# Moving the renewal of the residual stream from GpSimd to VectorE, and reordering the start of a mixer, in a two-layer trunk on one Trainium2 core

## The chip, the cores and the metric

The kernel runs on one core of one Trainium2 chip. The metric is the device time of one execution in microseconds (us). Five engines work side by side: PE (TensorE, matrix products), DVE (VectorE), ACT (ScalarE), POOL (GpSimd) and SP (SyncE, which issues the DMA transfers of the weights).

## The reference, cut to what matters

```
for layer in range(2):
    shift, scale, gate = ada_modulation(c, ada_w[layer, 0], ada_b[layer, 0])
    h = x * (1.0 + scale) + shift
    y = mixer_ab(h, ...) if layer == 0 else mixer_c(h, ...)
    x = layer_norm(DN_ALPHA * x + gate * y, ln_g[layer, 0], ln_b[layer, 0])
    shift, scale, gate = ada_modulation(c, ada_w[layer, 1], ada_b[layer, 1])
    h = x * (1.0 + scale) + shift
    y = squared_relu_mlp(h, mlp_w1[layer], mlp_w2[layer])
    x = layer_norm(DN_ALPHA * x + gate * y, ln_g[layer, 1], ln_b[layer, 1])
```

There are 256 tokens of width 1024, all in float32. `mixer_c` is causal attention over queries, keys and values that one projection `c_w_in` gives (16 heads of 64). The MLP is 1024 to 4096 to 1024. `ada_modulation` multiplies the vector c with a 1024 x 3072 matrix, four times in all.

## The kernel before

The tokens are two blocks b of 128. Every product of the trunk is float32 in three passes (`mm3`, L232 to L236): both factors are split into a high and a low part, ACT makes the high part by a cast (`wh`, `hTh`, `uh`, L171) and DVE the low one by a subtraction (`wl`, `hTl`, `ul`, L172).

**Weights.** `plan` is one list of keys of 1 MB each: `w1` and `w2` of an MLP, `ci` the input projection of mixer C (`ci` 0 and 1 queries of the first head group, 2 and 3 keys, 4 and 5 values), `ada` the modulation matrices. SP loads them in this order into four places. `take` consumes the next key: a weight is split, in two halves, into places for three keys; an `ada` key is two products on DVE (`ada_product`, L320, tile `junk`), with no work for PE. `need(key)` takes up to a key, `ahead(n)` takes n weights further. `LATER` moves single instructions earlier (negative) or later in the order that the scheduler writes for each engine; an engine runs its list in order.

**An MLP** (`mlp`, L911) has 16 steps i. Step i makes hidden units from `w1` (`first`) and adds the last step's to four accumulators in PSUM with `w2` (`second`), which for MLP 0 keeps products of block 1 back for its finish.

**Between two stages** each block b goes through `residual` (L570 to L572: z from the accumulator, gate and x, and its statistics), `moments` (a reciprocal root on POOL, L300) and `norm` (L587). PE transposes z (`ps_mod`, L421); ACT (L426) and for half of block 1 DVE (L429) evacuate it with scale and shift into `h`; ACT and DVE split it into `hTh` and `hTl`, which the next stage's products read. In `renew` (between MLP 0 and mixer C) this is written out in L596 to L608; after a mixer `mixed_out` does it beside the output products. The next residual needs x itself: `new_x` (L589) makes it from z with the LayerNorm's gain and shift (`lngB`, `lnbB`), in four multiplications and four additions of 128x512 on POOL, straight behind the norms. This happens three times: after mixer 0, after MLP 0 and after mixer C.

**Mixer C starts** with `c_project(0)` (L998): queries of blocks 0 and 1, then keys of blocks 0 and 1, then values.

Of the kernel before, what the change touches and what calls it, by code (L numbers as in the profile page):

```python
# [42 lines left out]
NSPLIT = 6  # L43

SPLITS_LATER, ADA_LATER, ROWS_LATER = 200, 300, 0
LATER = {("co", 1, 1): -300, ("wo", 2, 0): 400, ("ada", 1, 5): 500, "cM1": 30, "cO011": -300, "cO100": 100, "s1": -300, "wO010": 30, "wO110": -40, "wY10": -80}

BESIDE = {"a0": [2, 2, 2, 2], "a1": [2, 2, 2, 2], "b0": [2, 2, 2, 2], "c10": [3, 1, 1, 1]}

# [13 lines left out]
def trunk(ctx: ExitStack, tc, c, x, pos, small, ln, ada, w_g, w_g1, w_uq, w_out, c_in, c_out, w1, w2, out):  # L63
# [39 lines left out]
    def ada_ss(i):  # L103
        return [("ada", i, k) for k in range(8)]

    def ada_g(i):
        return [("ada", i, 8 + j) for j in range(4)]
# [5 lines left out]
        "ada_1_4 ada_1_5 ada_1_6 ada_1_7"  # L113
    ).split()]

    def mlp_plan(l, more):

        more, p = list(more), [("w1", l, 0)]
        for i in range(16):
            p += ([("w1", l, i + 1)] if i < 15 else []) + [("w2", l, i)]  # L120
            if i >= 2:
                take = -(-len(more) // 8)
                p += more[:take]
                more = more[take:]
        assert not more
        return p

    plan += mlp_plan(0, ada_g(1) + ada_ss(2) + ada_g(2))
    plan += [("ci", j) for j in range(6)]
    for j in range(6):  # L130
        plan += [("ci", 6 + j)] + ada_ss(3)[j:j + 1]
    plan += [("co", 0)] + ada_ss(3)[6:] + [("co", j) for j in (1, 2, 3)]
    plan += mlp_plan(1, ada_g(3))
    place = {key: i for i, key in enumerate(plan)}

    source = {"ada": lambda i, o: ada[i, o], "g": lambda k: w_g[k], "g1": lambda k: w_g1[k], "uq": lambda: w_uq,
# [32 lines left out]
    def split(dh, dl, src):  # L169

        nc.scalar.copy(dh, src)  # L171
        nc.vector.tensor_sub(dl, src, dh.bitcast(F32))  # L172

    def take():

        key = plan[state["taken"]]
        w = raw.get(key)
        if w is None:
            pass
        elif key[0] == "uq":  # L180
            parts[key] = [w[:, :1024], w[:, 1024:]]
        elif by_tensor(key):
            with later(ROWS_LATER):
                ada_rows(key, w)
        elif key[0] == "ada":
            j = state["half"]
            with later(LATER.get(key, ADA_LATER)):
                state["half"] = ada_product(key, j, w[:, j * D:(j + 1) * D])
            if state["half"]:
                return  # L190
        else:
            cuts = (0, 1024, 2048)
            parts[key] = []
            for part, (lo, hi) in enumerate(zip(cuts, cuts[1:])):
                if key in (("wo", 0), ("co", 0)):
                    if lo == 0:
                        wide = [t.rearrange("p k q -> p (k q)") for t in new_hT()]
                    wh, wl = wide[0][:, lo:hi], wide[1][:, lo:hi]
                else:
                    wh = sp.tile([P, 1024], F32R, name="wh", tag="wh")[:, :hi - lo]  # L200
                    wl = sp.tile([P, 1024], F32R, name="wl", tag="wl")[:, :hi - lo]
                half = (*key, part)
                with later(LATER.get(half, SPLITS_LATER)):
                    split(wh, wl, w[:, lo:hi])
# [237 lines left out]
    def rope(src, heads, b, dsts, eng=nc.vector):  # L442

        t1 = work.tile([P, 8, HD], F32, name="rope1", tag="r2", bufs=8)[:, :heads]
        t2 = work.tile([P, 8, HD], F32, name="rope2", tag="r2", bufs=8)[:, :heads]
        cs = cosT[:, b:b + 1, :].to_broadcast([P, heads, HD])
        lo = sinT[:, b:b + 1, :32].to_broadcast([P, heads, 32])
        hi = sinT[:, b:b + 1, 32:].to_broadcast([P, heads, 32])
        eng.tensor_mul(t1, src, cs)
        eng.tensor_mul(t2[:, :, :32], src[:, :, 32:], lo)  # L450
        eng.tensor_mul(t2[:, :, 32:], src[:, :, :32], hi)
        for d, view in dsts:
            eng.tensor_add(d, view(t1), view(t2))
# [110 lines left out]
    def new_z():  # L564
        return work.tile([P, D], F32, name="z", tag="w4", bufs=2), col([P, 2, 6], "stats")
# [21 lines left out]
            nc.vector.tensor_scalar(z[:, s], z[:, s], mv[:, 0:1], rs, op0=ALU.subtract, op1=ALU.mult)  # L587

    def new_x(zs, gb):  # L589
        for b in range(NB):  # L590
            for h in range(2):
                s = slice(h * 512, (h + 1) * 512)
                nc.gpsimd.tensor_mul(xt[b][:, s], zs[b][0][:, s], gb[0][:, s])
                nc.gpsimd.tensor_add(xt[b][:, s], xt[b][:, s], gb[1][:, s])

    def renew(finish, gb, i):  # L596

        need(("ada", i, 7))
        zs = [new_z() for b in range(NB)]
        hT = new_hT()  # L600
        for b in range(NB):
            finish(b, zs[b])
            norm(b, zs[b])
            modulate(zs[b][0], b, i, hT)
            if b == 0:
                ahead(1)
        new_x(zs, gb)
        return hT  # L608


    xT = [work.tile([P, 4, 256], F32, name=f"xT{h}", tag="w4", bufs=2) for h in range(2)]
# [233 lines left out]
    def mixed_out(ys, name, i, first, second, under_first, under_second, after):  # L845

        yT, accs, zs, got = [None, None], {}, {}, {}  # L850
        got["ln"] = ln_rows(i)

        def step(s):
            op, *n = s
            b = int(n[0]) if n else 0
            if op in todo:
                with later(LATER.get(s, 0)):
                    todo[op](b)
            if op == "Y":
                if n[1] == "0":  # L860
                    yT[b] = new_yT(b)
                with later(LATER.get(name[0] + s, 0)):
                    y_half(ys[b], yT[b], int(n[1]))
                if n[1] == "1":
                    zs[b] = new_z()
            elif op == "O":
                h, kq = int(n[1]), int(n[2])
                if (b, h) not in accs:
                    accs[b, h] = pa("ps_out")
                need((name, 2 * h + kq))  # L870
                with later(LATER.get(name[0] + s, 0)):
                    out_part(accs[b, h], yT[b], (name, 2 * h + kq), kq, kq == 0, kq == 1)
            elif op == "G":
                with later(LATER.get(name[0] + s, 0)):
                    got["gate"] = gate_row(i)
            elif op == "R":
                with later(LATER.get(name[0] + s, 0)):
                    residual(b, int(n[1]), accs[b, int(n[1])], got["gate"], zs[b])
            elif op == "N":
                with later(LATER.get(name[0] + s, 0)):  # L880
                    norm(b, zs[b])
            elif op == "M":
                if b == 0:
                    need(("ada", i + 1, 7))
                    got["h"] = new_hT()
                with later(LATER.get(name[0] + s, -100)):
                    modulate(zs[b][0], b, i + 1, got["h"])

        def go(todo):
            for group in todo.split("|"):  # L890
                for s in group.split():
                    step(s)
                yield

        together(first, go(under_first))
        together(second, go(under_second))
        together(go(after))

        def rest():
            step("M1")  # L900
            new_x([zs[0], zs[1]], got["ln"])

        return got["h"], rest

# [5 lines left out]

    def mlp(l, hT, rest, rows):  # L911
        held = l == 0
        acc = [[(pd if b else pa)("ps_m2") for h in range(2)] for b in range(NB)]
        us = {}

        def first(i):
# [9 lines left out]
            ul = work.tile([P, 512], F32R, name="ul", tag="r2", bufs=8)  # L926
            nc.scalar.activation(r, ps, AF.Relu)
            nc.scalar.activation(r, r, AF.Square)
            split(uh, ul, r)
            us[i] = uh, ul  # L930

        def first_tokens(i, b):
# [28 lines left out]
        need(("w1", l, 1))  # L961
        for i in range(2):
            first_tokens(i, 0)
        rest()
        for i in range(2):
            first_tokens(i, 1)
        for i in range(16):
            if i >= 1:
                need(("w2", l, i - 1))
            if i > 1:  # L970
                first(i)
            if i == 10:
                gB, gb = rows()
            if i < 15:
                need(("w1", l, i + 1))
            if 1 <= i < 15:
                for b in range(NB):
                    for h in range(2):
                        if not (held and b and i == 14):
                            second(i - 1, b, h)  # L980
# [11 lines left out]
        return finish, gb  # L992

    finish, gb = mlp(0, hT, rest, lambda: (gate_row(1), ln_rows(1)))
    hT = renew(finish, gb, 2)


    ys = [work.tile([P, D], F32, name=f"y{b}", tag="w4", bufs=2) for b in range(NB)]  # L998
# [1 line left out]
    def c_project(g, got):  # L1000
# [121 lines left out]
```

## Time and profile before

| | |
|---|---|
| time, median of 3 | 679.63 us (678.79 to 680.69) |
| the profiled execution | 681.17 us, span 679.4 us |
| granted clock of PE, mean | 0.979 of full speed |
| busy: PE, DVE, ACT, POOL | 640.7, 470.8, 339.8, 74.4 us |
| DMA queue of the weights | 150.71 MB, 60.8% of 16 engines |

The profile is of one execution; its span leaves out 1.8 us around the program. The stages lie as follows: mixer 0 up to about 150 us, MLP 0 up to 341, mixer C from there up to about 480, MLP 1 up to about 665, and the last LayerNorm. In the rows below an entry in brackets is the idle time of the engine ahead of the instruction, and what ended it.

### The profile page before, as it was taken

To read this page: it belongs to the slowest core of one execution; us is meant where nothing else is said; L and a number is where in the kernel's file an instruction comes from. 1 tells how busy PE (TensorE), PEld (TensorE's weight loads), DVE (VectorE), ACT (ScalarE), POOL (GpSimd) and SP (SyncE) were. 2 spreads that over 40 slices of the span, in tenths; PEclk is the share of its full clock that TensorE was granted. 3 is DMA by queue.
4 is the path that set the end of the run, shared out by engine and by line. 5 is a ranking of instruction groups with operands and counts; after the bars stand their busy time and mean duration, and the time that the engine had idled before them with its cause. 6 is when DMAs were issued, how large, how long until landed. Compare 5 with 4: busy or idle time off the path is not lost.

```text
span 679.4 us, 9863 instructions
## 1 busy us (share of the span) xinstructions
PE 640.7 (94%) x3802; PEld 531.7 (78%) x3802; DVE 470.8 (69%) x859; ACT 339.8 (50%) x538; POOL 74.4 (11%) x93
## 2 busy tenths in 40 slices
PE   6999988998999999999959999999999999999994
PEld 3545766876898989899847887888788989898983
DVE  2859877278888778665687889864986744445437
ACT  3326656264645554555443554782655454555440
POOL 4010003044020000000051000002410000000004
PEclk8999989999999999999977999999999999999997
DMA  8992678406798978775344775830568675545301
GB/s 304 409 414 103 211 265 326 192 4 244 276 380 306 352 271 316 294 291 206 110 173 155 277 291 212 304 124 1 177 215 312 246 254 184 198 157 190 113 1 62
DMA packets 24385, 151.52 MB, mean 223 GB/s; under 512 B 2833, under 2 KB 3089, under 8 KB 8338
## 3 DMA queue, kind: packets, MB, share of 16 engines
q1 hardware_dynamic: 24194, 150.71, 60.8%
q8 instruction: 30, 0.49, 0.3%
q10 hardware_dynamic: 144, 0.18, 0.1%
q14 instruction: 17, 0.14, 0.1%
HBM read 149.83 MB, written 1.05 MB: 222 GB/s over the span
## 4 chain that ended last, share of the span: by engine, by line
PE 75%; DVE 7%; issue 7%; DMA 5%; ACT 2%; POOL 2%; SPq 0%; DVEq 0%; POOLq 0%; ACTq 0%
PE ps_m L236 17%; PE ps_m L234 17%; PE ps_m L235 17%; PE ps_s L491 3%; PE ps_c L236 3%; PE ps_c L235 3%; PE ps_c L234 3%; PE ps_pv L510 3%; DMA w_ada<-in_ada_dram 3%; DVE wl L172 2%; PE ps_pt L503 2%; DMA w_g<-in_w_g_dram 2%; PE ps_ada L340 1%; DMA early<-in_ada_dram 1%; PE ps_T L469 1%
## 5 line engine op out<-in xcount | busy, mean ns | idle before, releaser
L172 DVE TENSOR_TENSOR wl<-w_w,wh 128x1024 fp32r<-128x1024 f32 x128 | 157.3, 1248 | 93.2 <-ACT wh L171 92.6
L171 ACT CAST wh<-w_w 128x1024 fp32r<-128x1024 f32 x128 | 131.1, 1052 | 154.7 <-PE ps_m L235 89.0
L234 PE MATMUL ps_m<-hTh,wh 128*128 128x256 f32 x448 | 126.7, 283 | 0.0
L236 PE MATMUL ps_m<-hTh,wl 128*128 128x256 f32 x448 | 126.7, 283 | 0.0
L235 PE MATMUL ps_m<-hTl,wh 128*128 128x256 f32 x448 | 126.6, 283 | 0.0
L234 PE MATMUL ps_m<-wh,uh 128*128 128x512 f32 x256 | 101.9, 399 | 0.0
L235 PE MATMUL ps_m<-wl,uh 128*128 128x512 f32 x256 | 101.4, 396 | 0.2 <-DVE wl L172 0.2
L236 PE MATMUL ps_m<-wh,ul 128*128 128x512 f32 x256 | 101.2, 397 | 0.0
L320 DVE CUSTOM_DVE_ANT_0 junk<-w_ada,cB,sm 128x1024 bf16<-128x1024 f32 x68 | 87.2, 1282 | 12.6 <-DMA w_ada<-in_ada_dram 11.7
L235 PEld LDWEIGHTS ps_m<-hTl,wh 128*128 128x128 f32 x448 | 85.7, 191 | 1.3
L234 PEld LDWEIGHTS ps_m<-hTh,wh 128*128 128x128 f32 x448 | 85.7, 191 | 1.2
L236 PEld LDWEIGHTS ps_m<-hTh,wl 128*128 128x128 f32 x448 | 85.7, 191 | 0.1
L236 PEld LDWEIGHTS ps_m<-wh,ul 128*128 128x128 f32 x256 | 48.2, 188 | 11.7 <-DVE ul L172 0.4
L234 PEld LDWEIGHTS ps_m<-wh,uh 128*128 128x128 f32 x256 | 48.3, 189 | 10.3 <-ACT uh L171 0.8
L235 PEld LDWEIGHTS ps_m<-wl,uh 128*128 128x128 f32 x256 | 48.3, 189 | 10.3 <-DVE wl L172 0.8
L236 PE MATMUL ps_c<-wh,hTl 128*128 128x512 f32 x96 | 39.9, 415 | 5.0 <-DVE hTl L172 5.0
L234 PE MATMUL ps_c<-wh,hTh 128*128 128x512 f32 x96 | 41.0, 427 | 3.2 <-ACT hTh L171 3.2
L300 POOL TENSOR_TENSOR rs<-rs,mhalf 128x1 f32<-128x1 f32 x8 | 6.7, 833 | 312.7 <-DVE rs L578 312.7
L235 PE MATMUL ps_c<-wl,hTh 128*128 128x512 f32 x96 | 39.7, 414 | 0.0
L171 ACT CAST wh<-w_ci 128x1024 fp32r<-128x1024 f32 x24 | 25.1, 1054 | 28.1 <-PE ps_c L236 20.3
L172 DVE TENSOR_TENSOR ul<-relu,uh 128x512 fp32r<-128x512 f32 (+1 forms) x36 | 24.8, 689 | 16.6 <-ACT uh L171 16.6
L172 DVE TENSOR_TENSOR wl<-w_ci,wh 128x1024 fp32r<-128x1024 f32 x24 | 31.2, 1309 | 7.1 <-ACT wh L171 6.8
(231 smaller groups left out, 1046.8 us busy)
## 6 DMA issues: line engine op xcount, KB each, us to landing
w_w<-in_w_dram SPq DMA_DIRECT2D x64, 1024.0 KB, 4.9
w_ada<-in_ada_dram SPq DMA_DIRECT2D x40, 1024.0 KB, 5.3
w_ci<-in_c_in_dram SPq DMA_DIRECT2D x12, 1024.0 KB, 4.8
w_ada<-in_ada_dram SPq DMA_DIRECT2D x12, 512.0 KB, 9.5
w_wo<-in_w_out_dram SPq DMA_DIRECT2D x4, 1024.0 KB, 5.5
w_co<-in_c_out_dram SPq DMA_DIRECT2D x4, 1024.0 KB, 4.9
w_g<-in_w_g_dram SPq DMA_DIRECT2D x8, 356.0 KB, 9.5
early<-in_ada_dram SPq DMA_DIRECT2D x4, 512.0 KB, 8.6
```

The source lines that it names most:

```text
L171: nc.scalar.copy(dh, src)
L172: nc.vector.tensor_sub(dl, src, dh.bitcast(F32))
L234: nc.tensor.matmul(ps, a[0], b[0], start=start, stop=False)
L235: nc.tensor.matmul(ps, a[0], b[1], start=False, stop=False)
L236: nc.tensor.matmul(ps, a[1], b[0], start=False, stop=stop)
L300: state["pow"] = nc.gpsimd.tensor_tensor(out=dst, in0=src, in1=mhalf, op=ALU.pow)
L320: state[key, j] = nc.vector.tensor_tensor_reduce(out=junk, in0=w, in1=cB, scale=1.0, scalar=bias, op0=ALU.mult, op1=ALU.add, accum_out=m)
L340: behind("pv", nc.tensor.matmul(ps[g, :256], cT[:, k:k + 1].to_broadcast([P, 32]), w[:, 256 * k:256 * (k + 1)], start=k < 4, stop=k >= 4))
L469: nc.tensor.transpose(ps[:, j * P:(j + 1) * P], s, ident)
L491: nc.tensor.matmul(ps[:, j * 256:j * 256 + nk], qT[:, p0 + j, b * P:(b + 1) * P], kT(p0 + j, half)[:, :nk], start=True, stop=True)
L503: nc.tensor.transpose(pt[:, o:o + P], pr[:, j, kb * P:(kb + 1) * P], ident)
L510: state["pv"] = nc.tensor.matmul(pv[:, i * 65:(i + 1) * 65], flat[:, o:o + P], vv(kb, head(p0 + j, half)), start=(kb == 0), stop=(kb == b))
```

## The change

`new_x` becomes a generator of eight instructions on DVE, each held behind the last rope or split that DVE did for the running work. Its steps are called for beside later products: in MLP 0 four at each of the steps i = 8 and 9, in `c_project(0)` two behind each product from the second on, in MLP 1 one at each of i = 3 to 10. The rows of the next gate and LayerNorm are therefore made at i = 13 and 12, not 10.

The first weights of an MLP, and the last of MLP 0, are split into places of the queries and keys. `renew` takes one weight more ahead of the finish, and `ci` 0 moves to the front of the order. `c_project(0)` does queries and keys of block 0 before those of block 1.

In `plan`, six of the eight `ada` keys that were loaded in mixer C go into MLP 0, which then has 22 in place of 16: two in each of i = 2 to 7 and 10 to 13, one in 8 and 9 (before, two in i = 2 to 5 and one from there). The memsets of the padded keys `ckT` stay on POOL.

```
-LATER = {("co", 1, 1): -300, ...
+LATER = {("ci", 0, 0): -1000, ("ci", 0, 1): -1000, ("co", 1, 1): -300, ...
+X_STEPS = ({8: 4, 9: 4}, 13), ({i: 1 for i in range(3, 11)}, 12)
...
-    plan += mlp_plan(0, ada_g(1) + ada_ss(2) + ada_g(2))
-    plan += [("ci", j) for j in range(6)]
-    for j in range(6):
-        plan += [("ci", 6 + j)] + ada_ss(3)[j:j + 1]
-    plan += [("co", 0)] + ada_ss(3)[6:] + [("co", j) for j in (1, 2, 3)]
-    plan += mlp_plan(1, ada_g(3))
+    plan += mlp_plan(0, ada_g(1) + ada_ss(2) + ada_g(2) + ada_ss(3)[:6], [0, 0] + 6 * [2] + 2 * [1] + 4 * [2] + [0, 0])
+    plan += [("ci", j) for j in range(8)] + ada_ss(3)[6:7] + [("ci", 8), ("ci", 9)] + ada_ss(3)[7:] + [("ci", 10), ("ci", 11)]
+    plan += [("co", j) for j in range(4)]
+    plan += mlp_plan(1, ada_g(3), [0, 0] + 4 * [1] + 10 * [0])
...
-                if key in (("wo", 0), ("co", 0)):
+                if key in (("w1", 0, 0), ("w1", 1, 0), ("w2", 0, 15)):
+                    wh, wl = (work.tile([P, 1024], F32R, name=n, tag="q4", bufs=5) for n in ("wh", "wl"))
+                elif key in (("wo", 0), ("co", 0)):
...
     def new_x(zs, gb):
...
-                nc.gpsimd.tensor_mul(xt[b][:, s], zs[b][0][:, s], gb[0][:, s])
-                nc.gpsimd.tensor_add(xt[b][:, s], xt[b][:, s], gb[1][:, s])
+                behind("vector", nc.vector.tensor_mul(xt[b][:, s], zs[b][0][:, s], gb[0][:, s]))
+                yield
+                behind("vector", nc.vector.tensor_add(xt[b][:, s], xt[b][:, s], gb[1][:, s]))
+                yield
...
     def renew(finish, gb, i):
 
         need(("ada", i, 7))
+        ahead(1)
...
-        new_x(zs, gb)
-        return hT
+        return hT, new_x(zs, gb)
...
-            if i == 10:
+            if i == at:
                 gB, gb = rows()
+            for _ in range(steps.get(i, 0)):
+                next(more)
...
-        for part in range(3):
-            for b in range(NB):
-                products(part, b)
+        for part, b in ([(0, 0), (1, 0), (0, 1), (1, 1)] if g == 0 else [(0, 0), (0, 1), (1, 0), (1, 1)]) + [(2, 0), (2, 1)]:
+            products(part, b)
...
+            if g == 0 and (part, b) != (0, 0):
+                for _ in range(2):
+                    next(more, None)
```

What stands in an engine's list is shown below with the line numbers of each kernel (those of the changed one are one higher from L232 to L588 and one lower in `split`).

On DVE, in `renew`, between the statistics of block 0 and those of block 1, the kernel before has:

```order
448 L570 TENSOR_TENSOR z<-ps_m_1458,gateB 128x512
449 L587 TENSOR_SCALAR z<-z,mv,rs 128x512 x2
450 L571 SCALAR_TENSOR_TENSOR z<-x_81,z 128x512
451 L172 TENSOR_TENSOR wl<-w_ci_3104,wh 128x1024
452 L572 BN_STATS stats<-z 128x6
453 L570 TENSOR_TENSOR z<-ps_m_1459,gateB 128x512
454 L172 TENSOR_TENSOR wl<-w_ci_3104,wh 128x1024
455 L172 TENSOR_TENSOR hTl<-h_3242,hTh 128x4x128
```

The changed kernel has (x_81 and ps_m_1458, ps_m_1459 are block 1, h_3242 and h_3297 block 0):

```order
480 L571 TENSOR_TENSOR z<-ps_m_1458,gateB 128x512
481 L577 BN_AGGR mv<-stats 128x2
482 L171 TENSOR_TENSOR wl<-w_ci_3161,wh 128x1024
483 L579 TENSOR_SCALAR rs<-mv 128x1
484 L572 SCALAR_TENSOR_TENSOR z<-x_81,z 128x512
485 L588 TENSOR_SCALAR z<-z,mv,rs 128x512 x2
486 L573 BN_STATS stats<-z 128x6
487 L571 TENSOR_TENSOR z<-ps_m_1459,gateB 128x512
488 L171 TENSOR_TENSOR wl<-w_ci_3161,wh 128x1024
489 L572 SCALAR_TENSOR_TENSOR z<-x_81,z 128x512
490 L171 TENSOR_TENSOR hTl<-h_3297,hTh 128x4x128
```

Block 0's aggregate and norm stand behind block 1's first residual now, and one split fewer stands ahead of `hTl`.

On PE, in mixer C, where block 1's z is transposed (ps_mod), the kernel before goes straight on to block 1's queries (ps_c_3409, which read the same weights wh_3261 as block 0's):

```order
1496 L235 MATMUL ps_c_3361<-wl_3379,hTh_3198 128x512
1497 L236 MATMUL ps_c_3361<-wh_3378,hTl_3199 128x512
1498 L421 MATMUL ps_mod_3320<-ident_132,z_3196 128x128 x4
1499 L421 MATMUL ps_mod_3332<-ident_132,z_3196 128x128 x4
1500 L234 MATMUL ps_c_3409<-wh_3261,hTh_3198 128x512
1501 L235 MATMUL ps_c_3409<-wl_3262,hTh_3198 128x512
```

In the changed kernel the keys of block 0 (ps_c_3446) come between, and block 1's queries are ps_c_3507:

```order
1497 L422 MATMUL ps_mod_3375<-ident_132,z_3251 128x128 x4
1498 L422 MATMUL ps_mod_3387<-ident_132,z_3251 128x128 x4
1499 L235 MATMUL ps_c_3408<-wh_3320,hTh_3253 128x512
1500 L236 MATMUL ps_c_3408<-wl_3321,hTh_3253 128x512
1501 L237 MATMUL ps_c_3408<-wh_3320,hTl_3254 128x512
1502 L236 MATMUL ps_c_3446<-wl_3448,hTh_3253 128x512
...
1512 L237 MATMUL ps_c_3446<-wh_3451,hTl_3254 128x512
1513 L235 MATMUL ps_c_3507<-wh_3239,hTh_3253 128x512
```

Fourteen products of block 0 stand between the transposes and block 1's first one.

On DVE in MLP 0, around the step i = 8, the changed kernel has both the new x (x_79 is block 0) and `ada` products between the splits:

```order
396 L171 TENSOR_TENSOR wl<-w_w_0_9_2327,wh 128x1024 x2
397 L171 TENSOR_TENSOR wl<-w_w_0_8_2361,wh 128x1024
398 L171 TENSOR_TENSOR ul<-relu,uh 128x512
399 L595 TENSOR_TENSOR x_79<-z,lngB 128x512 x2
400 L597 TENSOR_TENSOR x_79<-x_79,lnbB 128x512 x2
401 L171 TENSOR_TENSOR wl<-w_w_0_8_2361,wh 128x1024
402 L321 ISA junk,mod_171<-w_ada_8_2427,cB,sm 128x1024
403 L321 ISA mod_171 128x1
```

Before, these four instructions stood on POOL at the front of the stage.

## Rows read from the trace of the kernel before

**Rows 1.** The page: span and PE.

```profile
span 679.4 us, 9863 instructions
PE 640.7 (94%) x3802; PEld 531.7 (78%) x3802; DVE 470.8 (69%) x859; ACT 339.8 (50%) x538; POOL 74.4 (11%) x93
```

**Rows 2.** Timeline of PE, 338 to 360 us: instructions with idle time ahead.

```profile
342.60 0.51 PE L234 MATMUL ps_c<-wh,hTh 128*128 128x512 f32 x1 [1.36 <-ACT hTh L171]
347.38 0.80 PE L236 MATMUL ps_c<-wh,hTl 128*128 128x512 f32 x1 [4.04 <-DVE hTl L172]
357.09 0.50 PE L234 MATMUL ps_c<-wh,hTh 128*128 128x512 f32 x1 [1.81 <-ACT hTh L171]
358.81 0.80 PE L236 MATMUL ps_c<-wh,hTl 128*128 128x512 f32 x1 [0.98 <-DVE hTl L172]
```

**Rows 3.** Windows in `renew`: busy of PE, PEld, DVE, ACT, POOL; granted clock; DMA.

```profile
346.00:350.00 4.00, 2.62 (x6) 2.15 (x7) 4.00 (x6) 0.00 (x1) 0.00 (x0) 0.50 0.57 172
358.00:364.00 6.00, 5.19 (x15) 4.13 (x15) 3.94 (x6) 1.56 (x2) 1.15 (x2) 0.50 0.32 105
```

**Rows 4.** Timeline of PE: neighbouring products at either clock.

```profile
349.25 0.63 PE L234 MATMUL ps_c<-wh,hTh 128*128 128x512 f32 x1
349.68 0.63 PE L235 MATMUL ps_c<-wl,hTh 128*128 128x512 f32 x1
...
352.43 0.39 PE L235 MATMUL ps_c<-wl,hTh 128*128 128x512 f32 x1
352.66 0.39 PE L236 MATMUL ps_c<-wh,hTl 128*128 128x512 f32 x1
```

**Rows 5.** Timeline of POOL in `renew`: block 0's two multiplications of the new x.

```profile
338.99 3.20 POOL L593 TENSOR_TENSOR x<-z,lngB 128x512 f32<-128x512 f32 x2 [0.66 <-DVE z L587]
```

**Rows 6.** Timeline of DVE in `renew`.

```profile
340.99 2.28 DVE L172 TENSOR_TENSOR wl<-w_ci,wh 128x1024 fp32r<-128x1024 f32 x1
...
347.25 0.68 DVE L571 SCALAR_TENSOR_TENSOR z<-x,z 128x512 f32<-128x512 f32 x1
347.85 1.21 DVE L172 TENSOR_TENSOR wl<-w_ci,wh 128x1024 fp32r<-128x1024 f32 x1
```

**Rows 7.** Waits of PE at the front of MLP 0, 140 to 168 us.

```profile
PE ps_m L235 <- DVE wl L172: 1.5, 2, 0.8
PE ps_m L234 <- ACT hTh L171: 1.3, 1, 1.3
PE ps_m L236 <- DVE hTl L172: 1.2, 2, 1.0
PE ps_mod L421 <- DVE z L587: 0.4, 1, 0.4
PE ps_u L947 <- ACT relu L944: 0.2, 1, 0.2
```

**Rows 8.** Waits of PE at the front of MLP 1, 468 to 498 us.

```profile
PE ps_m L236 <- DVE hTl L172: 1.1, 1, 1.1
PE ps_mod L421 <- DVE z L587: 0.6, 2, 0.4
PE ps_m L234 <- ACT hTh L171: 0.4, 1, 0.4
PE ps_m L235 <- DVE wl L172: 0.2, 1, 0.2
```

**Rows 9.** Timeline of DVE at the front of MLP 0: the last split of block 1.

```profile
163.86 3.39 DVE L172 TENSOR_TENSOR hTl<-h,hTh 128x512 fp32r<-128x512 f32 x2
```

**Rows 10.** Windows of two steps of MLP 0 with two `ada` keys each, columns as in rows 3.

```profile
181.60:193.00 11.40, 11.40 (x74) 10.34 (x73) 10.12 (x14) 5.92 (x9) 0.00 (x0) 1.00 0.97 370
193.00:204.30 11.30, 11.30 (x74) 10.24 (x73) 9.41 (x13) 5.82 (x9) 3.83 (x5) 1.00 0.98 370
```

**Rows 11.** Waits of DVE in MLP 0, 170 to 300 us, the largest group.

```profile
DVE wl L172 <- ACT wh L171: 20.4, 19, 2.5
```

**Rows 12.** Timeline of DVE in MLP 0: an `ada` product.

```profile
184.57 1.28 DVE L320 CUSTOM_DVE_ANT_0 junk<-w_ada,cB,sm 128x1024 bf16<-128x1024 f32 x1
```

More of the change, by code (lines that the diff above doesn't have):

```diff
@@ L45 @@
 SPLITS_LATER, ADA_LATER, ROWS_LATER = 200, 300, 0
-LATER = {("co", 1, 1): -300, ("wo", 2, 0): 400, ("ada", 1, 5): 500, "cM1": 30, "cO011": -300, "cO100": 100, "s1": -300, "wO010": 30, "wO110": -40, "wY10": -80}
+LATER = {("ci", 0, 0): -1000, ("ci", 0, 1): -1000, ("co", 1, 1): -300, ("wo", 2, 0): 400, ("ada", 1, 5): 500, "cM1": 30, "cO011": -300, "cO100": 100, "s1": -300, "wO010": 30, "wO110": -40, "wY10": -80}
+X_STEPS = ({8: 4, 9: 4}, 13), ({i: 1 for i in range(3, 11)}, 12)
 BESIDE = {"a0": [2, 2, 2, 2], "a1": [2, 2, 2, 2], "b0": [2, 2, 2, 2], "c10": [3, 1, 1, 1]}
@@ L114, in trunk, with mlp_plan @@
     ).split()]
-    def mlp_plan(l, more):
+    def mlp_plan(l, more, room):
         more, p = list(more), [("w1", l, 0)]
         for i in range(16):
[L120 to L124, printed above, removed]
+            p += [("w1", l, j) for j in {13: (14, 15), 14: ()}.get(i, (i + 1,)) if j < 16] + [("w2", l, i)]
+            take = room[i]
+            p += more[:take]
+            more = more[take:]
         assert not more
         return p
-    plan += mlp_plan(0, ada_g(1) + ada_ss(2) + ada_g(2))
-    plan += [("ci", j) for j in range(6)]
-    for j in range(6):
-        plan += [("ci", 6 + j)] + ada_ss(3)[j:j + 1]
-    plan += [("co", 0)] + ada_ss(3)[6:] + [("co", j) for j in (1, 2, 3)]
-    plan += mlp_plan(1, ada_g(3))
+    plan += mlp_plan(0, ada_g(1) + ada_ss(2) + ada_g(2) + ada_ss(3)[:6], [0, 0] + 6 * [2] + 2 * [1] + 4 * [2] + [0, 0])
+    plan += [("ci", j) for j in range(8)] + ada_ss(3)[6:7] + [("ci", 8), ("ci", 9)] + ada_ss(3)[7:] + [("ci", 10), ("ci", 11)]
+    plan += [("co", j) for j in range(4)]
+    plan += mlp_plan(1, ada_g(3), [0, 0] + 4 * [1] + 10 * [0])
     place = {key: i for i, key in enumerate(plan)}
@@ L171, in split @@
         nc.scalar.copy(dh, src)
-        nc.vector.tensor_sub(dl, src, dh.bitcast(F32))
+        return nc.vector.tensor_sub(dl, src, dh.bitcast(F32))
     def take():
@@ L452, in rope @@
         for d, view in dsts:
-            eng.tensor_add(d, view(t1), view(t2))
+            state["vector"] = eng.tensor_add(d, view(t1), view(t2))
     plain = lambda t: t
@@ L900, in rest @@
             step("M1")
-            new_x([zs[0], zs[1]], got["ln"])
+            return new_x([zs[0], zs[1]], got["ln"])
         return got["h"], rest
@@ L912, in mlp @@
         held = l == 0
+        steps, at = X_STEPS[l]
         acc = [[(pd if b else pa)("ps_m2") for h in range(2)] for b in range(NB)]
@@ L928, in first @@
             nc.scalar.activation(r, r, AF.Square)
-            split(uh, ul, r)
+            state["vector"] = split(uh, ul, r)
             us[i] = uh, ul
@@ L963, in mlp @@
             first_tokens(i, 0)
-        rest()
+        more = rest()
         for i in range(2):
@@ L994, in trunk @@
     finish, gb = mlp(0, hT, rest, lambda: (gate_row(1), ln_rows(1)))
-    hT = renew(finish, gb, 2)
+    hT, more = renew(finish, gb, 2)
     ys = [work.tile([P, D], F32, name=f"y{b}", tag="w4", bufs=2) for b in range(NB)]
@@ L1017, in products @@
                 b_rope(ps, ([qT], kT)[part], b)
-        for part in range(3):
-            for b in range(NB):
-                products(part, b)
-                if b == 1:
-                    ahead(1)
-                yield
+        for part, b in ([(0, 0), (1, 0), (0, 1), (1, 1)] if g == 0 else [(0, 0), (0, 1), (1, 0), (1, 1)]) + [(2, 0), (2, 1)]:
+            products(part, b)
+            if b == 1:
+                ahead(1)
+            if g == 0 and (part, b) != (0, 0):
+                for _ in range(2):
+                    next(more, None)
+            yield
     def c_attend(g, got, blocks=range(NB)):
```

## The prediction

> **What bounds the kernel now.** I read the page first. PE is busy for 640.7 of 679.4 us [rows 1], so a change can only be worth something where PE waits or runs slow, and the most there is to win anywhere is 38.7 us plus what a lower clock costs. Next I looked for the stretches in which PE waits. Inside MLP 0 the windows of two steps show PE busy for the whole of both, at 11.40 and 11.30 us, although DVE works for 10.12 and 9.41 us of them [rows 10]; nothing is to be won there, but something can be lost. The waits lie where one stage hands over to the next, and I read each hand-over by its list of PE instructions with idle time ahead, or by its groups of waits.
>
> In `renew`, between MLP 0 and mixer C, PE waits 1.36 + 4.04 us for block 0's split and 1.81 + 0.98 us for block 1's: 8.2 us [rows 2]. Behind both, PE's clock is granted at 0.50, the lower of its two levels, 1.2 GHz [rows 3]. Neighbouring products then start 0.43 us apart instead of 0.23 us [rows 4], 0.20 us lost for each. At least the six of the first window and the 15 of the second run so: 1.2 + 3.0 = 4.2 us. `renew` costs 12.4 us in all.
>
> At the front of MLP 0 PE waits 1.5 + 1.3 + 1.2 + 0.4 + 0.2 = 4.6 us [rows 7], at the front of MLP 1 1.1 + 0.6 + 0.4 + 0.2 = 2.3 us [rows 8], with the clock at its full 2.4 GHz in both.
>
> In all three places POOL makes the new x while DVE is on the path. In `renew` its first two instructions fill 338.99 to 342.19 us [rows 5], and a DVE split that starts at 340.99 us takes 2.28 us, where the same split at 347.85 us, with POOL idle, takes 1.21 us [rows 6]. The pair of `hTl` at the front of MLP 0 takes 3.39 us [rows 9]; two of the 0.68 us that such an instruction of 128x512 takes alone [rows 6] are 1.4 us.
>
> **The change part by part.**
>
> *New x on DVE.* It removes POOL's 24 instructions and so the slowing of DVE, and puts 24 instructions of 128x512 on DVE. The trace has no such instruction on DVE with this form; the nearest, the residual with both inputs in the same memory, takes 0.68 us and the next starts 0.60 us later [rows 6]. I take 0.6 us, with 0.68 as the upper end; 24 are 14 to 16 us in all, 4.8 in each stage. The lower end is that all of it lies in idle time of DVE. None is waited for by the stage in which it runs: x is next read a stage later.
>
> *Front of MLP 0.* The splits `wl` fall from 2.3 to 1.2 us, so the 1.5 us of waits for them go. The pair of `hTl` is 2 us shorter; its wait of 1.0 us becomes about 0.3, and block 0's of 0.2 goes. The wait for `hTh` (1.3 us) comes from ACT behind the transposes and stays, as do z and relu. What stays is about 2.3 us; gain 2.2 us (1.5 to 3.5).
>
> *Front of MLP 1.* The same, with 1.1 us falling to 0.3 and the 0.2 us gone: gain 1.0 us (0.5 to 1.8).
>
> *`renew`, block 0.* Two things go against each other. Block 0's norm stands behind block 1's first residual in DVE's order and all products of MLP 0 stand ahead of the transposes on PE, where five covered the wait before. From the end of the accumulator ps_m_1458, behind which PE has the last 12 products of ps_m_1459 or 2.8 us, DVE does a residual step (0.6), the aggregate and a split (1.3), the root on POOL with its way there and back (1.2) and a norm half (0.5): 3.7 us, so PE waits 0.9 us ahead of the transposes. From the first transpose (339.04 us) to the first product (342.60 us) it was 3.56 us; the transposes themselves take 1.04, so up to 2.4 us more of waiting, with nothing to cover it. But the 4.04 us of waiting for `hTl` nearly goes: two slowed splits and a residual stood ahead of it, and now it is due about 0.7 us after `hTh`, while two or three products are run: 0.1 us. Sum 3.4 us against 5.4.
>
> *`renew`, block 1.* Fourteen products of block 0 stand behind its transposes now, 14 x 0.23 = 3.2 us, which with the 1.04 us of transposes covers the 4 us that `hTh` took from the first transpose. The wait of 1.81 us goes; `hTl` leaves 0.3 us of 0.98, and the transposes may wait 0.7 us for the norm. Sum 1.0 us against 2.8. Idle time of `renew` then falls from 8.2 to 4.4 us: gain 3.8 us.
>
> *The clock.* The pair of waits of block 0 (3.3 us with eight short transposes between) is shorter than the 5.4 us behind which the clock fell, but of the size of block 1's 2.8 us behind which it also fell, and larger than the pair at the front of MLP 0 (1.3 + 1.0 us), behind which it did not. So I take one fall at 3.0 us and none behind block 1: gain 1.2 us, with 4.2 (no fall) and 0 as ends.
>
> *First weights in other places, the other order of C, `ci` 0 early.* They make the fourteen products and the early splits possible; cost of their own: none is issued more than before. The keys of block 0 want `ci` 3 while block 1 still needs `ci` 0 and 1, and there are split places for three keys. The order puts half of block 1's queries ahead; `ci` 3's first half then has 6 products (1.4 us) for a cast of 1.05 us. I take nothing, with 5 us as the other end.
>
> *`ada` keys into MLP 0.* Six keys more, 12 products of about 1.3 us [rows 12], 16 us of DVE, and the 4.8 us of new x. Twelve steps then ask DVE for 4 x 1.2 (`wl`) + 0.6 (`ul`) + 4 x 1.3 = 10.6 us (10.4 where x replaces a key) out of 11.35. Two steps of that kind ran with PE full [rows 10]. I take nothing; the other end is the slower rival. What leaves mixer C is worth nothing, since PE has no waits there to speak of.
>
> Sum: 2.2 + 1.0 + 3.8 + 1.2 = 8.2 us, and an estimated 0.5 us for the drains and refills of PE around five waits that vanish (0.1 us each: the first product in the pairs of [rows 4] stays 0.63 or 0.39 us in PE, longer than the 0.43 or 0.23 us to the next): 8.7 us. The profiled execution took 681.17 us, which gives 672.5; it is 1.5 us above the median, and 679.63 - 8.7 = **670.9 us** is what I forecast.
>
> **The rivals.**
>
> *No fall of the clock in `renew`* (0.23): 3.0 us more, 667.9 us. For it speaks that MLP 0's front had 2.3 us of waits in a row and kept the full clock.
>
> *`ci` 3 comes too late* (0.12): PE waits in the middle of block 0's keys for a cast and a split, some 2.5 us, and the clock falls again, 3.0 us: 676.4 us. For it speaks that each place is freed only by a product that runs just before.
>
> *Transfers bind MLP 0* (0.06): a step with two `ada` keys moves 4 x 1.049 MB, at 11.35 us 370 GB/s, which is just what the two windows show, at a DMA share of 0.97 and 0.98 [rows 10]. If over ten such steps only 352 GB/s are to be had, a step lasts 11.9 us, and 5.5 us are lost: 676.4 us. The Trainium skill, "DMA: Bandwidth & Descriptors", section "Where 436 GB/s comes from", names about 358 GB/s as what binds one core's transfers from HBM; an estimate by it would be 11.7 us a step, 3.5 us lost and 674.4 us. The trace does not agree: it shows 370 GB/s.
>
> *DVE binds MLP 0* (0.08), the one that ends slower. DVE idles in front of `wl` for ACT's cast, 19 times for 20.4 us [rows 11]. With w us of such waits in a step, DVE falls behind by 10.6 + w - 11.35 us. Split weights are three keys ahead and a step uses two, a lead of 17 us. Over twelve steps the lead lasts up to w = 2.2 us; at w = 3.1 us PE loses 28 - 17 = 11 us: 682 us. Rows 10 leave 1.3 and 1.9 us for w, which speaks against. The Trainium skill, "Perfetto Trace Analysis", section "Optimizing Scalar/DVE Operations", advises to move work off a saturated DVE, which is the reverse of this change, but adds that the two engines share a read port, so that it might not help; with the second half the trace agrees, by the split of 2.28 us.
>
> *Nothing comes of it* (0.05): the longer wait for `hTh` eats what the others give, the clock falls twice as before: 679 us.
>
> **How the numbers follow.** My forecast has 0.46. The four cases of 670.9, 667.9 and twice 676.4 us are all faster by over 0.3% (2 us, about what a measurement here can tell): 0.87. Same 0.05, slower 0.08. The low end takes the case without a fall and the upper ends of both fronts (1.3 + 0.8 us more): 665.5; the high end takes the two cases of 676.4 us: 677. The likeliest case alone is 668.8 to 673, by the same ends of the fronts and 2 us for `ci` 3.
>
> **What would show it.** POOL without its 128x512 instructions at the three hand-overs; DVE's `wl` at 1.2 us throughout them; a wait for `hTl` of block 0 in `renew` below 0.5 us, for `hTh` at about 2.4 us, block 1's both below 0.5 us; at most one window at 0.50; MLP 0's steps still 11.35 us long. Steps above 11.5 us, or PE waits for `wl` or `wh` in MLP 0, would make the forecast wrong; so would a wait of PE for `wh` of `ci` 3.

## The result and the profile after

The changed kernel takes 670.42 us (median of 4, 669.14 to 671.51) against 680.16 us of the kernel before on the same chip: a ratio of 0.9853, 95% interval 0.982 to 0.9886. The forecast was 670.9 us. That the total came out so near is partly luck, as the terms show.

The page of the profile after (the execution of 671.51 us), where [rows 1] had PE at 640.7 us and POOL at 74.4:

```profile
span 669.7 us, 9853 instructions
PE 637.4 (95%) x3802; PEld 531.2 (79%) x3802; DVE 469.4 (70%) x883; ACT 339.9 (51%) x538; POOL 36.9 (6%) x69
PEclk9999978999999999999999999999999999999998
```

POOL has 24 instructions fewer and half its busy time, DVE 24 more. DVE's busy time is even 1.4 us lower, since what it was slowed by is gone. In the third row, slices of 17 us, the clock is below full in slices 6 and 7, mixer 0; `renew` (slices 20 to 22) is at full clock.

PE with idle time ahead, 325 to 372 us, the answer to [rows 2]:

```profile
341.07 1.08 PE L422 MATMUL ps_mod<-ident,z 128*128 128x128 f32 x8 [0.97 <-DVE z L588]
344.15 0.50 PE L235 MATMUL ps_c<-wh,hTh 128*128 128x512 f32 x1 [1.99 <-ACT hTh L170]
350.48 1.11 PE L422 MATMUL ps_mod<-ident,z 128*128 128x128 f32 x8 [0.91 <-DVE z L588]
355.61 0.47 PE L235 MATMUL ps_c<-wh,hTh 128*128 128x512 f32 x1 [0.82 <-DVE rope L452]
```

No wait for `hTl` is left, and none for block 1's `hTh`. Two waits are new, 0.97 and 0.91 us ahead of the transposes, and one nobody reckoned with, 0.82 us for a rope: 4.7 us in all, where it was 8.2.

DVE and POOL in the same stretch (start, duration, line, output and inputs), beside [rows 6]:

```profile
344.22 0.69 DVE L171 TENSOR_TENSOR hTl<-h,hTh 128x512 fp32r<-128x512 f32 x1
...
345.43 1.21 DVE L171 TENSOR_TENSOR wl<-w_ci,wh 128x1024 fp32r<-128x1024 f32 x1
...
349.18 1.70 DVE L588 TENSOR_SCALAR z<-z,mv,rs 128x512 f32<-128x512 f32 x2 [0.67 <-POOL rs L301]
```

```profile
349.20 0.95 POOL L1012 MEMSET ckT__3690<- 64x1024 f32 x1
```

The split takes 1.21 us where it took 2.28. But block 1's norm, two halves that take 1.00 us elsewhere, takes 1.70 us just while POOL clears a padded key.

The waits of PE at the front of MLP 0 (138 to 172 us) and MLP 1 (455 to 500 us), the answers to [rows 7] and [rows 8]: summed us, count, longest.

```profile
PE ps_m L235 <- ACT hTh L170: 1.4, 2, 0.9
```

```profile
PE ps_m L235 <- ACT hTh L170: 1.1, 1, 1.1
PE ps_mod L422 <- DVE z L588: 0.5, 2, 0.3
```

1.4 us stay of 4.6, and 1.6 of 2.3. Inside MLP 0 PE has no wait. Two of its steps after, in the columns of [rows 10]:

```profile
226.64:237.13 10.49, 10.49 (x70) 9.60 (x69) 9.97 (x16) 4.90 (x8) 0.00 (x0) 1.00 0.93 365
259.78:271.94 12.16, 12.16 (x77) 10.94 (x76) 12.08 (x16) 6.69 (x8) 0.00 (x0) 1.00 0.83 301
```

These are the two steps in which DVE is busiest, 95% and 99% of the time; PE does not wait. Of twelve steps, eight last 11.33 us, as before. One lasts 12.42 us, for it has the products of the gate row; before, another step had them. The remaining three (10.49, 12.16 and 10.50 us) differ because products moved between them, and four products of MLP 0 now run in its finish. So it is not DVE that makes the second one longer: PE works through all of it, on 76 products in place of 72.

Last, mixer 0, whose part at 93 us no term of the forecast touched. Windows of the changed kernel, and then of the kernel before:

```profile
96.00:98.00 2.00, 2.00 (x20) 0.99 (x18) 1.66 (x10) 1.14 (x3) 0.00 (x0) 0.50 0.20 82
98.00:100.00 2.00, 2.00 (x15) 1.51 (x8) 0.00 (x0) 0.67 (x2) 0.00 (x0) 0.50 0.50 70
```

```profile
96.00:98.00 2.00, 2.00 (x18) 1.03 (x18) 1.75 (x10) 1.19 (x3) 0.00 (x0) 0.50 0.27 111
98.00:100.00 2.00, 2.00 (x21) 1.48 (x14) 0.16 (x1) 0.67 (x2) 0.00 (x0) 0.86 0.31 41
```

In both the clock falls to its lower level (1.2 GHz); before, it is back within the second window (at 98.6 us), after, only at 107 us. The same transposed probabilities (`probT`, ACT) are evacuated at 119.48 us before and 123.34 after, 3.9 us later.

### The profile page after: what moved, and what is told of

Same layout as the page of the kernel before. It is cut to its first block, busy times and chain, and to the rows that moved or that the text cites. A ratio compares the mean times of both kernels' runs of the same rounds, so it can differ in the third digit from the quotient of the medians.

```text
span 669.7 us, 9853 instructions
## 1 busy us (share of the span) xinstructions
PE 637.4 (95%) x3802; PEld 531.2 (79%) x3802; DVE 469.4 (70%) x883; ACT 339.9 (51%) x538; POOL 36.9 (6%) x69
## 5 line engine op out<-in xcount | busy, mean ns | idle before, releaser
L171 DVE TENSOR_TENSOR wl<-w_w,wh 128x1024 fp32r<-128x1024 f32 x128 | 153.7, 1222 | 75.8 <-ACT wh L170 75.5
L235 PE MATMUL ps_c<-wh,hTh 128*128 128x512 f32 x96 | 38.8, 407 | 2.8 <-ACT hTh L170 2.0
L236 PE MATMUL ps_c<-wl,hTh 128*128 128x512 f32 x96 | 38.3, 401 | 0.0
L237 PE MATMUL ps_c<-wh,hTl 128*128 128x512 f32 x96 | 38.0, 396 | 0.0
L171 DVE TENSOR_TENSOR ul<-relu,uh 128x512 fp32r<-128x512 f32 (+1 forms) x36 | 22.7, 630 | 21.9 <-ACT uh L170 21.9
L500 ACT ACTIVATE prob<-prob,negm 128x128 f32<-128x128 f32 (+1 forms) x64 | 27.3, 455 | 20.0 <-DVE negm L496 19.7
L171 DVE TENSOR_TENSOR wl<-w_ci,wh 128x1024 fp32r<-128x1024 f32 x24 | 28.6, 1216 | 4.1 <-ACT wh L170 4.0
```

The lines of the kernel that those rows point to most:

```text
L171: return nc.vector.tensor_sub(dl, src, dh.bitcast(F32))
L235: nc.tensor.matmul(ps, a[0], b[0], start=start, stop=False)
L236: nc.tensor.matmul(ps, a[0], b[1], start=False, stop=False)
L237: nc.tensor.matmul(ps, a[1], b[0], start=False, stop=stop)
L500: state["exp"] = nc.scalar.activation(pr[:, j, :nk], pr[:, j, :nk], AF.Exp, bias=negm[:, hd:hd + 1], scale=-1.0)
```

## The experiments

Ratios are to the kernel before on the same chip, with 95% intervals. The kernels of one group below shared their runs of the kernel before; the very last was run by itself.

### First group: engine, order, repetition

**New x back on POOL, straight behind the norms.**

```
-  behind("vector", nc.vector.tensor_mul(xt[b][:, s], ...))
+  nc.gpsimd.tensor_mul(xt[b][:, s], ...)      # the addition likewise
...
+  for _ in more:        # all eight at once, in mlp and in renew
+      pass
```

> The changed kernel with the new x back on POOL, straight behind the norms as before; all else changed. Theory (GpSimd slows VectorE at the three hand-overs): the waits of PE for hTl and wl come back, about 3 us at the front of MLP 0, 0.7 us at that of MLP 1 and 2 to 4 us in renew, and the clock falls in renew again: 675 to 678 us. Rival (the early weights and the new order give the gain, GpSimd beside VectorE costs nothing): within 1 us of the changed kernel, 669.5 to 671.5 us.

682.81 us, 1.0029 [1.0003, 1.0054]: the whole gain is gone, and more than I expected. In `renew`, PE, POOL and DVE:

```profile
349.32 0.50 PE L235 MATMUL ps_c<-wh,hTh 128*128 128x512 f32 x1 [2.01 <-ACT hTh L170]
...
363.36 0.47 PE L235 MATMUL ps_c<-wh,hTh 128*128 128x512 f32 x1 [2.09 <-DVE rope L452]
```

```profile
346.17 5.05 POOL L595 TENSOR_TENSOR x<-z,lngB 128x512 f32<-128x512 f32 x2 [0.66 <-DVE z L588]
```

```profile
352.22 1.76 DVE L171 TENSOR_TENSOR hTl<-h,hTh 128x512 fp32r<-128x512 f32 x1
...
359.65 2.90 DVE L171 TENSOR_TENSOR hTl<-h,hTh 128x512 fp32r<-128x512 f32 x2
```

Both engines slow each other: two multiplications take 5.05 us on POOL where they took 3.20 [rows 5], and the `hTl` pair 2.90 us where it takes 1.29 in the changed kernel. At the front of MLP 0 PE waits 2.9 us for `hTl` and 1.9 for others, and the clock, full there in both other profiles, falls twice (155.7 to 159.1 and 169.4 to 172.8 us). The mechanism of the theory held, though not its 675 to 678 us, and the rival fell: with the new x on POOL the rest of the change is worth nothing.

**New x on POOL, called for late.** The same two lines on POOL without the loop.

> The changed kernel with the new x on POOL, but at the late places (MLP 0 at i = 8 and 9, c_project(0), MLP 1 at i = 3 to 10). Theory (what counts is that the new x leaves the hand-over, not the engine): PE is full at the late places in any case, so slowed splits are hidden: 669.5 to 672 us. Rival (work on GpSimd beside VectorE costs wherever it runs): at least a third of what the front costs, 672 to 676 us, with waits of PE for wl in MLP 0 or in c_project(0).

682.08 us, 1.0018 [0.9992, 1.0045]. It did not test what it should: POOL had nothing else in its list and ran x at 149.42 and 346.18 us, straight behind the norms. It is a second measurement of the kernel above; the next group holds x back by a wait.

**Old order of `c_project(0)`.**

```
-  for part, b in ([(0, 0), (1, 0), (0, 1), (1, 1)] if g == 0 else [(0, 0), (0, 1), (1, 0), (1, 1)]) + ...
+  for part, b in [(0, 0), (0, 1), (1, 0), (1, 1)] + ...
```

> The changed kernel with the old order of c_project(0): queries of blocks 0 and 1, then keys. Theory (fourteen products of block 0 behind the transposes cover block 1's hTh): the wait for hTh of block 1 comes back at about 2 to 2.8 us, and with it perhaps a fall of the clock worth 3 us; the wait of 0.8 us for the rope goes: 671.5 to 676 us. Rival (with VectorE free of GpSimd block 1 is early enough): within 1 us of the changed kernel.

671.16 us, 0.9869 [0.984, 0.9899], against 671.28 of the changed kernel on the same chip: no difference, so the theory fell. PE's wait ahead of block 1's queries changes its cause and hardly its size:

```profile
350.58 1.10 PE L422 MATMUL ps_mod<-ident,z 128*128 128x128 f32 x8 [0.88 <-DVE z L588]
351.44 0.48 PE L235 MATMUL ps_c<-wh,hTh 128*128 128x512 f32 x1
351.76 0.39 PE L236 MATMUL ps_c<-wl,hTh 128*128 128x512 f32 x1
351.99 0.40 PE L237 MATMUL ps_c<-wh,hTl 128*128 128x512 f32 x1
353.49 0.50 PE L235 MATMUL ps_c<-wh,hTh 128*128 128x512 f32 x1 [1.10 <-ACT hTh L170]
```

1.10 us for `hTh` in place of 0.82 for the rope that empties the accumulator which block 1's queries need.

**The changed kernel again.** No edit.

> The changed kernel once more, for the fall of the clock in mixer 0 that lasted from 93 to 107 us in its profile and from 95 to 99 us before. Theory (its length is chance, since the instructions there are the same): it is shorter in this profile or lies elsewhere, and the span is shorter by what it is shorter. Rival (the change makes it longer): it lasts 14 us again. Time 669 to 671.5 us by both.

671.28 us, 0.9873 [0.9833, 0.9913], span 669.2 us. In mixer 0 the clock is low from 96.4 to 106.6 us, 10 us and not 14, and the stage's marks come 0.6 us earlier than in the first profile. So the length varies from one execution of a program to the next; why is open. In the profiles of the other kernels of the study mixer 0 has one or two falls, of 3.4 to 14 us each, between 89 and 122 us.

### Second group: parts alone

**New x on DVE alone**, the rest as before (old plan, split places, `ci` 0 and order).

> The kernel before with one part of the change alone: the new x on VectorE at the late places (and the gate rows later, as they must be). Plan, first weights, early ci 0 and the order of c_project(0) as before. Theory (since the new x back on GpSimd cost 11 us, the new x is nearly the whole gain): 671 to 673.5 us, fronts of the MLPs as in the changed kernel, PE's wait for hTl of block 0 in renew below 1.5 us, no fall of the clock there. Rival (the early weights carry renew, since the splits of ci 0 and 1 stand ahead of hTl on VectorE): 674 to 677 us, with a wait for hTl of 2 us or more and a fall of the clock in renew.

671.5 us, 0.984 [0.9802, 0.9878], with single runs from 665.8 to 674.24. The theory held for the time, but not for the clock in `renew`:

```profile
343.19 0.50 PE L236 MATMUL ps_c<-wh,hTh 128*128 128x512 f32 x1 [1.29 <-ACT hTh L173]
344.68 0.50 PE L238 MATMUL ps_c<-wh,hTl 128*128 128x512 f32 x1 [0.75 <-DVE hTl L174]
351.01 1.11 PE L423 MATMUL ps_mod<-ident,z 128*128 128x128 f32 x8 [1.04 <-DVE z L589]
353.91 0.79 PE L236 MATMUL ps_c<-wh,hTh 128*128 128x512 f32 x1 [1.80 <-ACT hTh L173]
```

`hTl` is down from 4.04 us [rows 2] to 0.75. Behind the last two waits the clock falls for about 7 us, as in the kernel before. At the front of MLP 0 (138 to 172 us) these waits stay:

```profile
PE ps_m L236 <- ACT hTh L173: 1.3, 1, 1.3
PE ps_mod L423 <- DVE z L589: 0.4, 1, 0.4
PE ps_m L237 <- DVE wl L174: 0.3, 1, 0.3
PE ps_u L952 <- ACT relu L949: 0.2, 1, 0.2
```

That is 2.2 of 4.6 us [rows 7], and at the front of MLP 1 0.9 of 2.3 us [rows 8]: the waits for `hTl` are gone from both.

**New x on POOL, held back.** Each instruction waits for DVE's rope or split that it stood behind:

```
+  def beyond(what, m):
+      tc.add_manual_dep(m.ins, state[what].ins.name, ...)
...
-  behind("vector", nc.vector.tensor_mul(xt[b][:, s], ...))
+  beyond("vector", nc.gpsimd.tensor_mul(xt[b][:, s], ...))      # the addition likewise
```

> The changed kernel with the new x on POOL, and each of its instructions made to wait for the rope or split of VectorE behind which it stood on VectorE, so that it does run late (without that wait POOL ran it straight behind the norms). Theory (what counts is that it leaves the hand-over): 669.5 to 672 us, with PE full at the late places though splits there take up to 2.3 us. Rival (GpSimd beside VectorE costs wherever it runs): 673 us or more, with waits of PE in MLP 0, c_project(0) or MLP 1.

674.93 us, 0.9918 [0.9897, 0.9939]: most of the gain comes back with x still on POOL, once it leaves the hand-over. In MLP 0 it is hidden: PE has no wait though two instructions take 4.45 us. In `c_project(0)` and just behind it, it is not:

```profile
249.86 4.45 POOL L600 TENSOR_TENSOR x<-z,lngB 128x512 f32<-128x512 f32 x2 [52.14 <-DVE ul L171]
```

```profile
367.91 0.66 PE L475 MATMUL ps_T<-ident,qr 128*128 128x128 f32 x4 [0.79 <-DVE qr L459]
...
386.15 0.33 PE L509 MATMUL ps_pt<-ident,prob 128*128 128x128 f32 x1 [2.25 <-ACT prob L505]
```

The first of these waits is for a rope step (`qr`) that takes 1.79 us beside POOL and 0.68 without; the last stands behind three splits that take 5.69 us. Each theory was right in one place: where DVE stands between two of PE's steps, GpSimd beside it costs.

**New x on DVE, straight behind the norms.** The loop of the first experiment, without its change of engine.

> The changed kernel with the new x on VectorE, but straight behind the norms: four instructions of 0.6 us for each block between the splits of the hand-over. Theory (the place counts and not the engine): part of the 11 us comes back, since 2.4 us for each block lie on VectorE's way to hTl: 673 to 676 us. Rival (only GpSimd's slowing of VectorE counts): within 1 us of the changed kernel, 669.5 to 671.5 us.

677.25 us, 0.9943 [0.9925, 0.9961], so the place does count: the four instructions of block 1 stand ahead of the rope, and PE loses more than anywhere else, with a fall of the clock behind it.

```profile
357.36 0.76 PE L235 MATMUL ps_c<-wh,hTh 128*128 128x512 f32 x1 [4.21 <-DVE rope L452]
```

The two cases on POOL and on DVE at the front and the two late ones order themselves: 682 (POOL, front), 677 (DVE, front), 675 (POOL, late), 671 us (DVE, late). The intervals of the two in the middle overlap.

**Old plan**: 16 `ada` keys in MLP 0 and eight in mixer C (`plan` and `mlp_plan` of the kernel before, which also put the last `w1` of each MLP back behind a `w2`), all else changed.

> The changed kernel with the plan of the kernel before: 16 ada keys in MLP 0, eight in mixer C. Theory (PE is full in MLP 0 and in mixer C with either): within 1 us of the changed kernel, 669.5 to 671.8 us; the wait of PE for negm of 1.2 us in mixer C may go or move. Rival (without the six keys VectorE is freer at the end of mixer C than with them): 672 to 674 us, with more waits of PE for VectorE in mixer C.

668.7 us, 0.9822 [0.9801, 0.9842]: neither theory, it looks faster. Its interval overlaps those of the changed kernel, which was not run beside it; the two profiles, whose falls of the clock in mixer 0 are equally long, differ by 2.3 us (spans of 667.4 and 669.7), and PE's waits from MLP 0 on by 3.1. PE and DVE in `renew`:

```profile
341.96 0.50 PE L238 MATMUL ps_c<-wh,hTh 128*128 128x512 f32 x1 [1.24 <-ACT hTh L173]
343.52 0.50 PE L240 MATMUL ps_c<-wh,hTl 128*128 128x512 f32 x1 [0.36 <-DVE hTl L174]
347.68 1.11 PE L425 MATMUL ps_mod<-ident,z 128*128 128x128 f32 x8 [0.92 <-DVE z L591]
```

```profile
335.72 0.20 DVE L580 BATCH_NORM_AGGREGATE mv<-stats 128x2 f32<-128x12 f32 x1
...
336.99 0.68 DVE L574 TENSOR_TENSOR z<-ps_m,gateB 128x512 f32<-128x512 f32 x1
337.80 1.00 DVE L591 TENSOR_SCALAR z<-z,mv,rs 128x512 f32<-128x512 f32 x2
```

Block 0's aggregate stands ahead of block 1's residual again, so its norm does not wait for PE to finish the accumulator ps_m_1458, and five products of MLP 0 cover part of the wait for `hTh`. `renew` loses 2.5 us, not 4.7. PE's wait for `negm` in mixer C, 1.2 us in the changed kernel, is 0.4. So the new plan was not free: not by DVE's load in MLP 0, where PE has no wait with either plan, but because it shifted the scheduler's list in `renew`. Which part of the plan shifted it, the six keys or the `w1` moved up, no run tells.

### Third and fourth group: what is left

**Old plan and old order.**

> The changed kernel with the plan of the kernel before and the old order of c_project(0); against the new x alone (671.5 us) it adds only the first weights in other places and ci 0 and 1 early, against the old plan with the new order (668.7 us) it lacks the order. Theory (the early weights give the 3 us between these two, the order nothing, as with the new plan): 668 to 670 us, with the waits of the transposes' side in renew like those with the new order and PE's wait for block 1's hTh about 1.1 us. Rival (with the old plan the order does count, the early weights do not): 670.5 to 672.5 us, with a fall of the clock in renew.

667.95 us, 0.9789 [0.9774, 0.9803]. The new order gives nothing here either (with it 0.9822). Against the new x alone (0.984) the early weights give some 3 us, seen in `renew`: its waits are 1.25, 0.80 and 0.92 us, at full clock, where the new x alone has 4.9 us and a fall. The two were not run side by side, and their intervals just touch.

**Old plan, and the second group's memset held behind a rope.**

```
+  if g == 1:
+      beyond("vector", m)      # a wait for DVE's last rope, as above
```

> The changed kernel with the plan of the kernel before, and the memset of the second group's padded keys made to wait for the rope behind which it is written, so that it leaves block 1's norm. Theory (the memset on POOL slows the two norm halves on VectorE from 1.0 to 1.7 us, and PE waits for them): the norm takes 1.0 us, PE's wait of 0.92 us ahead of block 1's transposes falls to about 0.3: 667.5 to 668.3 us. Rival (the norm's two halves are slow for another reason): they still take 1.7 us, and the time stays at 668.7 us within 0.5.

667.66 us, 0.9782 [0.9759, 0.9804].

```profile
346.64 1.00 DVE L596 TENSOR_SCALAR z<-z,mv,rs 128x512 f32<-128x512 f32 x2 [0.66 <-POOL rs L304]
```

```profile
347.24 1.11 PE L430 MATMUL ps_mod<-ident,z 128*128 128x128 f32 x8 [0.21 <-DVE z L596]
```

With the memset gone (at 372 us now) the norm takes 1.00 us and PE waits 0.21 us, not 0.92: the mechanism is shown. The 0.7 us is too small for the times to settle.

**Four more multiplications on DVE in each of the steps 2 to 13 of MLP 0.**

```
+  behind("vector", nc.vector.tensor_mul(more_work[:, :512], xt[0][:, :512], xt[0][:, :512]))
```

> The changed kernel with four more multiplications of 128x512 on VectorE in each of the steps i = 2 to 13 of MLP 0, which nothing reads: about 2.4 us a step on top of 10.6. Theory (the lead of split weights is three keys or 17 us, and without it VectorE at 13 us and more a step sets the pace): PE waits for wl in MLP 0 and the time grows by 10 to 18 us, to 680 to 688 us. Rival (VectorE has more room than its list says, since it can run behind up to the end of MLP 0 and ada products can slip): less than 5 us more.

709.66 us, 1.0407 [1.0387, 1.0427]: some 37 us more than the changed kernel by the ratios, above all that I expected. Waits of PE in MLP 0:

```profile
PE ps_m L237 <- DVE wl L171: 16.9, 8, 4.4
PE ps_bt L389 <- POOL bc L387: 4.2, 1, 4.2
PE ps_m L235 <- ACT wh L170: 3.1, 4, 1.7
```

PE's first wait comes at 220.68 us, behind the step i = 5. The 48 instructions of 0.6 us are 29 us of DVE work; PE waits 24 us in MLP 0, where the changed kernel has no wait, and there are falls of the clock on top (four in MLP 0, one in `renew`). So neither the lead of 17 us that I reckoned with nor idle time of DVE took up more than some 5 us of them.

**Old plan, old order, late memset.**

> The changed kernel with the plan and the order of the kernel before and the late memset: new x on VectorE, first weights in other places, ci 0 and 1 early. Theory (the memset's 0.7 us lies on PE's way to block 1's queries, whose wait it shortens, and the order is worth nothing): 0.3 to 1 us below the old plan with the old order, a ratio to the kernel before of 0.976 to 0.979. Rival (with the old order block 1's hTh is waited for next, so the 0.7 us only moves into that wait): the same ratio as without it, 0.979 or more, with a longer wait for hTh of block 1.

666.48 us, 0.9776 [0.9746, 0.9806], the fastest version of the study. PE has no wait of note for block 1 in `renew`. Against 0.9789 without the late memset the difference is within the intervals. Its waits for block 0, 1.24 and 0.81 us, are those of the kernel without it, but here the clock falls behind them, from 341 to 345 us.

## Why the prediction was right, point by point

**New x on DVE, and the fronts.** Right in mechanism: it leaves POOL, DVE is no longer slowed, and by the first and second group it carries the gain (0.984 alone, nothing without). The Trainium skill, "SBUF — State Buffer", section "Who interferes with whom", says that a DVE instruction with two SBUF inputs contends with a GpSimd instruction that reads SBUF. The trace agrees: the split with both inputs there takes 2.28 us beside POOL and 1.21 without.

The front of MLP 0 came out larger: 3.2 us of waits went, not 2.2 (its own terms, 1.5 + 0.7 + 0.2, are 2.4). The new x alone is the forecast to the point, 4.6 to 2.2 us, with the waits for `hTh`, z and relu left. That those for z and relu went too came with the other parts, most likely the first weights in other places: the old plan with the old order has them but not the new plan or order, and its 1.4 us there are those of the changed kernel. The front of MLP 1 gave 0.7 and not 1.0: the new x alone took 1.4 off, and the other parts cost 0.7 of it.

**`renew`, block 0.** Right: 0.97 + 1.99 us, forecast 0.9 + 2.4 + 0.1 (the path of 3.7 us adds up to 3.6 from its terms, and 3.56 less 1.04 is 2.5, not 2.4). That DVE's list makes the norm wait for the accumulator ps_m_1458 is shown by the old plan, where it does not and the waits are 1.6 us.

**`renew`, block 1.** The step failed in part. The fourteen products do cover `hTh`, but little of the gain is the new order's: in the old order the wait is 1.10 us and not 1.81, because three products of block 0 stand behind the transposes there too and cover 0.7 us. That DVE is free of GpSimd has no part in it: with the new x alone, where none stands there, the wait is 1.80 us as before. What I left out is that block 1's queries need an accumulator that only a rope empties: with it the sum was 1.7 us, forecast 1.0. The 0.7 us ahead of the transposes was 0.91, most of it from the memset, by the old plan without it (0.92 to 0.21).

**The clock in `renew`.** The step "one fall at 3.0 us" was wrong for this execution: there was none, the case that had 0.23. The 4.2 us were a floor too, since they count only the products in two windows; the two falls last from 344.3 to 351.2 and 358.0 to 364.8 us, and the starts of all products in them give 4.6. The falls alone are therefore worth 3 us or more beyond the 1.2 us taken. Whether the clock falls behind waits of 2 to 3 us is not read from their size: two kernels with the same 1.25 and 0.80 us differ in it.

**First weights and early `ci`.** Taken at nothing; with the old plan they give some 3 us. **The plan.** Taken at nothing; it costs about as much, 0.9853 and 0.9873 against 0.9822 (the intervals overlap; the waits carry the reading), for the reason shown above and for the wait for `negm`, whose cause is open. The two about cancel in the changed kernel, so the total shows neither.

**The sum.** From MLP 0's last step to MLP 1's first full one (the evacuations of hidden units at 326.04 and 501.01 us, before at 327.18 and 510.68) the profiles differ by 8.5 us; of these 3.5 are waits in `renew`, 0.7 waits in MLP 1's front, less 1.0 for `negm`; 4.6 are the clock, and four products of MLP 0 that run in this stretch now take 0.9 back. The 1.6 left are, in the main, refills of PE. Mixer 0's longer fall of the clock took 3.6 us back by the start of MLP 0, and the front of MLP 0 gave 3.9; the other 0.8 us are those four products, which left the steps of MLP 0 and are no gain. The measured 9.7 us came near the forecast of 8.7 since a gain that I put too low met a loss that I did not see and that other executions have in other lengths: that is luck. How long mixer 0's fall lasts in the executions without a profile is not known. The low end of the range, 665.5, should be 665.8 by its terms.

**The rivals.** `ci` 3 too late: no wait for `wh` in `c_project(0)`. Transfers: PE is full in MLP 0 at 365 GB/s, and its twelve steps together are no longer than before. DVE bound: did not happen, but its price was wrong by the loaded kernel: there PE waited soon after DVE's list was longer than a step, and the changed kernel stands near that point in its two fullest steps, at 95% and 99%.

## What to carry to other kernels

Work that nobody waits for is dear if it runs beside the engine that everybody waits for: first move it out of the hand-over, then choose its engine. An edit that only moves loads and their products can move a norm in another engine's list by 2 us, so read the list at the hand-overs and price each part of a change alone; here two parts cancelled. Do not count split weights as a lead until a loaded run shows that PE rides on them.

## What was not expected of the hardware

A memset of 64x1024 on POOL, which reads nothing, slows two DVE instructions with one tensor input each from 1.00 to 1.70 us. The Trainium skill, "SBUF — State Buffer", section "Who interferes with whom", allows for it: a tensor_scalar can run in a mode that uses the port pair shared with GpSimd, and then contends. The trace agrees, by 1.00 us without the memset.

The clock of PE fell in mixer 0 for 3.4 us in the profile before, and for 14 and 10 us in two profiles of one program. It stayed full in `renew` behind 0.97 and 1.99 us of waits around eight transposes.
